# A streaming logsumexp on one core: tiles 42 to 53 weighed and summed by fused VectorE steps, and one wide constant matmul in place of three narrow ones

## The chip, the cores and the metric

The kernel runs on one core of a Trainium2 chip. The time is the device time of one execution in microseconds (us); what is compared is the median of several executions. The names used below are those of the profile: PE is TensorE's matmul, PEld its weight load, DVE is VectorE, ACT is ScalarE, POOL is GpSimd, SP is the SyncE queue that issues the DMAs.

## The reference

```python
# x: (8, 2048, 2048) float32, bias: (8, 256) float32; H = 8 heads of Dh = 256
x_heads = x.reshape(B, S, H, Dh).transpose(0, 2, 1, 3) + bias[None, :, None, :]
x_tiled = np.repeat(x_heads, 2, axis=2)          # each row twice
mx = x_tiled.max(axis=-1, keepdims=True)
lse = mx.squeeze(-1) + np.log(np.exp(x_tiled - mx).sum(axis=-1))   # (8, 8, 4096)
```

For every row of 2048 numbers there are eight sums of 256 exponentials, and the logarithm of each. The kernel leaves the maximum out, since the inputs are small; it checks at its end that no sum went out of range, and has a second, slow path for that case, which is not taken here.

## The kernel before

The input, 134 MB, is streamed through SBUF once, in 64 tiles of 2 MB: 128 partitions, K = 2 rows each, 2048 columns. There are eight tile buffers (NBUF). Tile t uses buffer t mod 8, and the load of tile t + 8 is issued by SP (`load`, L174 and L186) once the last user of tile t is done; the list `last_uses` says who that is. Loads are of two tiles (4 MB) up to tile 41 and of one tile or less after it. From tile 57 on a tile is loaded and worked by single rows, called units here; the last tile comes in eight pieces of columns (`LAST_COLS`).

The order of the work on every engine is the order in which the program emits it; nothing is reordered. `STAGES` gives each tile a mode. In a mode, `pe` is the number of heads whose bias TensorE adds, `g0` is the head from which GpSimd adds the bias, `acc` is the number of heads whose sum ScalarE makes itself while it takes the exponential, and heads from `pe` to `g0` get no bias at all: their exponentials are multiplied by exp(bias) afterwards, which is meant by "weighed". `fold` heads are weighed and half summed by GpSimd.

- BULK, tiles 0 to 53. TensorE puts the bias of heads 0 to 2 into PSUM (`put_bias`, L303) and adds x to it through a matmul on the identity (`late_heads`, L362). ScalarE takes the exponential of head 0 with its sum (L373) and of heads 1 and 2 without (L380). GpSimd adds the bias to heads 4 to 7 in place (`g_add`, L412). One tile later, in `later`, ScalarE takes the exponential of heads 3 to 7 in place (L418), VectorE multiplies head 3 of both rows by its factor (L430) and then sums heads 1 to 7 of both rows in one reduction of 3584 elements per partition (L437).
- MIXED, tiles 54 to 56. Head 0 goes through TensorE (`add_x`, L338; ScalarE L393). Heads 1 to 3 are weighed and summed by one fused VectorE step for each head and row (`weigh`, L453: multiply by the factor and accumulate). Heads 4 to 7 go as in BULK, but with a reduction of 2048 elements.
- Units of tiles 57 to 63. No GpSimd addition; TensorE takes the first heads, `weigh` the middle ones, and GpSimd weighs and folds the last one or two (`fold`, L469 and L477), which a short reduction finishes (L483).

At tile 54 `first_factors` makes the factors of heads 1 and 2 in the bank `one_ps`: TensorE spreads the bias over the partitions (L235) and ScalarE takes the exponential (L268). On TensorE this follows the bias matmul of tile 55, and on ScalarE it stands ahead of everything of tile 54.

From tile 57 on, `keep_warm` (L353) issues NWARM = 3 matmuls of the identity with itself for each unit, into the bank `tp`, where nobody reads them. `finish` transposes the sums of a batch into `tp` (L497), ScalarE takes their logarithm (L507); `finish_last` (L606, L612) does so for the last batch, and `ends_of` and `judge` (L525 to L550) test the range.

Of the kernel before, what the change touches and what calls it, by code (L numbers as in the profile page):

```python
# [13 lines left out]
ALU = mybir.AluOpType  # L14
# [7 lines left out]
NBUF = 8  # L22

NEARLY = 5

NWARM = 3

# [1 line left out]

BULK = dict(pe=3, acc=1, g0=4, late=True, fold=0)
MIXED = dict(pe=1, acc=1, g0=4, late=False, fold=0)
PROMPT_F1 = dict(pe=2, acc=2, g0=8, late=False, fold=1)
PROMPT_F2 = dict(pe=2, acc=2, g0=8, late=False, fold=2)
# [9 lines left out]

STAGES = [
    (0, (BULK,)),
    (54, (MIXED,)),  # L50
    (57, (PROMPT_F1, PROMPT_F1)),
    (62, (SINGLE_F1, SINGLE_F1)),
# [10 lines left out]
def kernel(  # L63
# [6 lines left out]
    nc = tc.nc  # L70
    P = nc.NUM_PARTITIONS
    B, S, D = x.shape
    H, Dh = bias.shape
# [2 lines left out]
    NB = S // (P * KB)  # L76
    TB = KB // K
    T = B * NBLK
    T_PROMPT = STAGES[1][0]
    T_FACTORS = T // 2  # L80
    CPE = BULK["pe"] * Dh
    MM = 512


    V0, W0, G0, W1, W2 = Dh, 3 * Dh, 4 * Dh, 6 * Dh, 7 * Dh
# [30 lines left out]
    xts = [xb[:, k : k + K] for xb in xbs for k in range(0, KB, K)]  # L116
    w_ps = pp.tile([P, W2 - W0], F32, name="w_ps")
# [5 lines left out]
    tp = pp.tile([P, KB, P], F32, name="tp")  # L123
# [41 lines left out]
    last_uses = [[] for _ in range(T)]  # L165
# [73 lines left out]
    for i, c in enumerate(range(G0, D, MM)):  # L239
        spread(ps[i], c, c + MM)  # L240
        nc.vector.tensor_copy(b_rep[:, c - G0 : c - G0 + MM], ps[i])
    W_LATE = BULK["g0"] * Dh
    w_late = w_ps[:, 0 : W_LATE - W0]
# [7 lines left out]
        out=b_far,  # L251
        in_=brow,
        op=ALU.max,
        axis=mybir.AxisListType.X,
# [3 lines left out]
        out=Rx[0][0:1, 1 + NR :],  # L258
# [90 lines left out]
        return heads  # L349

    def keep_warm():
        for _ in range(NWARM):
            nc.tensor.matmul(  # L353
                tp[:, 0], lhsT=ident, rhs=ident, start=True, stop=True
            )

    def late_heads(m, t, got, sums):


        mms = []  # L360
        for h, p in enumerate(got[:-1]):
            mm = nc.tensor.matmul(  # L362
                p,
                lhsT=ident,
                rhs=xts[t % NBUF][:, :, h * Dh : (h + 1) * Dh],
                start=False,
                stop=True,
            )
            mms.append(on_x(t, mm, [loads[t, 0, 0]]))

        def pe_part():
            for k in range(K):
                act = nc.scalar.activation(  # L373
                    out=xts[t % NBUF][:, k, 0:Dh],
                    in_=got[0][:, k * Dh : (k + 1) * Dh],
                    func=ACT.Exp,
                    accum_out=sums[:, k, 0:1],
                )
                last_uses[t].append(on_x(t, act, [mms[0]]))
            act = nc.scalar.activation(  # L380
                out=xts[t % NBUF][:, :, Dh : m["pe"] * Dh].rearrange(
                    "p k (h j) -> p h k j", j=Dh
                ),
                in_=got[-1].rearrange("p (h k j) -> p h k j", k=K, j=Dh),
                func=ACT.Exp,
            )
            on_x(t, act, [mms[-1]])

        return pe_part

# [26 lines left out]
    def exp_inplace(t, v, after):  # L417
        return on_x(t, nc.scalar.activation(out=v, in_=v, func=ACT.Exp), [after])  # L418

    def later(m, t, k0, k1, sums, add):  # L420

        h0 = m["pe"] if m["late"] else m["g0"]
        v = xts[t % NBUF][:, k0:k1, h0 * Dh : D]
        done = exp_inplace(t, v, add)
        if m["late"]:
            n = (m["g0"] - h0) * Dh
            f = v[:, :, 0:n]
            h0 = m["acc"]
            v = xts[t % NBUF][:, k0:k1, h0 * Dh : D]
            mul = nc.vector.tensor_tensor(  # L430
                out=f,
                in0=f,
                in1=each_row(w_ps, m["pe"] * Dh - W0, n, k1 - k0),
                op=ALU.mult,
            )
            done = on_x(t, mul, [done])
        red = nc.vector.tensor_reduce(  # L437
            out=sums[:, k0:k1, h0:H],
            in_=v.rearrange("p k (h j) -> p k h j", j=Dh),
            op=ALU.add,  # L440
            axis=mybir.AxisListType.X,
        )
        last_uses[t].append(on_x(t, red, [done]))

    def weigh(t, v, h, dst, after):
        c = h * Dh
        if c < W0:
            w = one_ps[:, c - V0 : c - V0 + Dh]
        elif c < W2:
            w = w_ps[:, c - W0 : c - W0 + Dh]  # L450
        else:
            w = w_sb[:, c - W1 : c - W1 + Dh]
        ttr = nc.vector.tensor_tensor_reduce(  # L453
            out=v,
            in0=v,
            in1=w,
            scale=1.0,
            scalar=0.0,
            op0=ALU.mult,
            op1=ALU.add,  # L460
            accum_out=dst,
        )
        last_uses[t].append(on_x(t, ttr, [after]))
# [181 lines left out]
    for t in range(T):  # L645
        if t == T_FACTORS:
            other_factors()
        xt = xts[t % NBUF]
        sums = sums_of(t)
        for k0, k1, c0, c1 in pieces(t):  # L650
            m = modes_of(t)[k0]
            add = None
            heads = []
            if c0 == 0:
                bias_here = bias_there
            if m["late"]:
                pe_part = late_heads(m, t, bias_here, sums)
            else:
                heads = add_x(m, t, k0, c0, c1, bias_here)

                def pe_part(t=t, heads=heads, sums=sums):
                    for k, h, bank, p, mm in heads:
                        sum_biased(t, k, h, bank, p, mm, sums)

            if c0 == 0:
                if next_units and not m["late"]:
                    bias_there = put_bias(*next_units.pop(0))
                if t > T_PROMPT and m["g0"] == H:
                    keep_warm()
                if m["g0"] < H:  # L670
                    add = g_add(m, t, k0, k1)
                if t < T - 1 or k0 == 0:
                    flush(for_pool)
            if t == T_PROMPT and (k0, c0) == (0, 0):
                first_factors()
            h0 = max(c0 // Dh, m["pe"])
            h1 = min(c1 // Dh, m["g0"])
            hf = max(h0, min(h1, H - m["fold"]))
            if h0 < h1 and not m["late"]:
                done = exp_inplace(  # L680
                    t, xt[:, k0:k1, h0 * Dh : h1 * Dh], loads[t, k0, c0]
                )
# [14 lines left out]

            def pool_part(t=t, m=m, k0=k0, k1=k1, sums=sums, add=add):
                if add:
                    later(m, t, k0, k1, sums, add)  # L700
# [56 lines left out]
```

## Time and profile before

| what | value |
|---|---|
| median of 3 runs | 326.36 us (325.95 to 326.98) |
| the profiled execution | 327.41 us, its span 325.5 us |
| DVE busy | 289.4 us, 89% of the span |
| POOL busy | 287.5 us, 88% |
| PE busy | 272.7 us, 84% |
| ACT busy | 265.6 us, 82% |
| DMA | 135.44 MB, mean 416 GB/s, 98.0% of 16 engines' span on the load queue |

The span is the time from the first to the last instruction of the program on the core; 1.9 us of the profiled execution's own time lie outside it. Four engines and the DMA are all busy for more than four fifths of the span, so shares alone do not tell which of them sets the end: that has to be read from the chain of waits and from the stretches late in the trace.

### The profile page before, as it was taken

The page shows a single profiled execution, that of the slowest core. Times are in us where ns is not written, and L with a number is a line of the kernel's source. Part 1 is how long each engine was busy: PE and PEld are TensorE (multiplying, and loading weights), DVE is VectorE, ACT ScalarE, POOL GpSimd, SP SyncE. Part 2 cuts the span into 40 slices and gives each one's busy share as a digit, 9 for nine tenths or more (in the row PEclk, how much of TensorE's full clock was granted, in tenths as well). Part 3 has the DMA queues.
Part 4 walks back from the last instruction along what each step waited for, and adds up shares of the span by engine and source line. Part 5 has one row for each costly group of instructions (what it writes and reads, how often), then busy time and mean ns, then how long its engine had stood idle before and what let it go on. Part 6 is the DMA issues. An engine that isn't in the chain of part 4 may idle for free.

```text
span 325.5 us, 2458 instructions
## 1 busy us (share of the span) xinstructions
PE 272.7 (84%) x695; PEld 102.8 (32%) x695; DVE 289.4 (89%) x329; ACT 265.6 (82%) x426; POOL 287.5 (88%) x120
## 2 busy tenths in 40 slices
PE   5999999878898869888688878698999786598983
PEld 2333333322233323332233323233333232135451
DVE  1346879999999998989989999969999999999996
ACT  1157789898598987889889979869899699989993
POOL 6939997999999899999999999999999999858872
PEclk9977899999597997979899979778999799589999
DMA  8999999999999999999999999999999999999992
GB/s 307 464 403 439 451 417 420 447 439 407 443 443 408 437 435 431 423 439 432 419 443 434 415 443 431 407 433 427 427 421 430 429 424 424 417 421 415 421 391 93
DMA packets 8832, 135.44 MB, mean 416 GB/s; under 512 B 1041, under 2 KB 1425, under 8 KB 2417
## 3 DMA queue, kind: packets, MB, share of 16 engines
q1 hardware_dynamic: 8720, 135.27, 98.0%
q8 instruction: 5, 0.08, 0.1%
q14 instruction: 9, 0.07, 0.1%
q10 hardware_dynamic: 98, 0.01, 0.0%
HBM read 134.23 MB, written 1.05 MB: 416 GB/s over the span
## 4 chain that ended last, share of the span: by engine, by line
DVE 43%; DMA 26%; PE 18%; ACT 8%; POOL 3%; issue 0%; SPq 0%; DVEq 0%
DVE R L437 28%; DMA xb<-in_x_dram 26%; DVE xb L453 9%; PE pair L362 7%; ACT xb L418 6%; DVE xb L430 4%; PE one_ps L362 4%; POOL xb L412 3%; PE pair L303 3%; PE one_ps L303 2%; PE pair L235 1%; ACT xb L380 1%; ACT xb L373 1%; DMA brow<-in_bias_dram 1%; ACT res L507 1%
## 5 line engine op out<-in xcount | busy, mean ns | idle before, releaser
L412 POOL TENSOR_TENSOR xb<-xb,b_rep 128x2048 f32<-128x2048 f32 x57 | 257.3, 4537 | 21.3 <-DMA xb<-in_x_dram 21.1
L437 DVE TENSOR_REDUCE R<-xb 128x14 f32<-128x3584 f32 (+1 forms) x57 | 216.8, 3804 | 1.9
L418 ACT ACTIVATE xb<-xb 128x2560 f32<-128x2560 f32 (+5 forms) x77 | 157.5, 2055 | 8.2 <-POOL xb L412 8.0
L362 PE MATMUL pair<-xb,ident 128*128 128x512 f32 x216 | 117.3, 671 | 0.0
L362 PE MATMUL one_ps<-xb,ident 128*128 128x512 f32 x108 | 68.1, 716 | 10.9 <-DMA xb<-in_x_dram 10.9
L380 ACT ACTIVATE xb<-pair 128x1024 f32<-128x1024 f32 x54 | 56.0, 1038 | 25.0 <-PE pair L362 25.0
L362 PEld LDWEIGHTS pair<-xb,ident 128*128 128x128 f32 x216 | 47.0, 218 | 62.6 <-issue 62.6
L430 DVE TENSOR_TENSOR xb<-xb,w_ps 128x512 f32<-128x512 f32 x54 | 36.8, 681 | 24.0 <-ACT xb L418 23.9
L373 ACT ACTIVATE xb<-one_ps 128x256 f32<-128x256 f32 x108 | 40.4, 387 | 6.7 <-PE one_ps L362 6.7
L303 PEld LDWEIGHTS <-ones 3*128 3x128 bf16 (+1 forms) x192 | 16.8, 95 | 78.0 <-issue 69.0
L303 PE MATMUL one_ps<-b,ones 3*128 3x512 bf16 x49 | 19.1, 390 | 20.9 <-ACT xb L373 20.9
L303 PE MATMUL pair<-b,ones 3*128 3x512 bf16 x98 | 29.1, 376 | 0.0
L362 PEld LDWEIGHTS one_ps<-xb,ident 128*128 128x128 f32 x108 | 17.2, 201 | 33.7 <-DMA xb<-in_x_dram 17.3
L338 PE MATMUL pair<-xb,ident 128*128 128x512 f32 (+1 forms) x36 | 20.5, 656 | 6.3 <-DMA xb<-in_x_dram 6.3
L373 ACT ACTIVATION_READ_ACCUMULATOR xb<-one_ps 128x1 f32 x108 | 23.0, 213 | 0.0
L453 DVE CUSTOM_DVE_ANT_0 xb<-xb,w_ps 128x256 f32<-128x256 f32 x61 | 22.3, 416 | 0.0
L477 POOL TENSOR_TENSOR xb<-xb 128x128 f32<-128x128 f32 (+3 forms) x39 | 13.9, 357 | 3.1
L469 POOL TENSOR_TENSOR xb<-xb,w_sb 128x256 f32<-128x256 f32 (+1 forms) x13 | 10.0, 772 | 5.2 <-ACT xb L418 4.6
L353 PE MATMUL tp<-ident 128*128 128x128 f32 x84 | 13.0, 291 | 0.9 <-ACT res L507 0.9
L507 ACT ACTIVATE res<-tp 32x1024 f32<-32x1024 f32 x7 | 7.1, 1011 | 6.2 <-PE tp L497 6.2
L393 ACT ACTIVATE xb<-pair 128x256 f32<-128x256 f32 x33 | 12.0, 368 | 0.0
L353 PEld LDWEIGHTS tp<-ident 128*128 128x128 f32 x84 | 10.5, 191 | 4.3 <-issue 2.8
(55 smaller groups left out, 91.8 us busy)
## 6 DMA issues: line engine op xcount, KB each, us to landing
xb<-in_x_dram SPq DMA_DIRECT2D x20, 4096.0 KB, 21.3
xb<-in_x_dram SPq DMA_DIRECT2D x17, 2048.0 KB, 22.0
xb<-in_x_dram SPq DMA_DIRECT2D x12, 1024.0 KB, 21.3
xb<-in_x_dram SPq DMA_DIRECT2D x4, 256.0 KB, 13.3
out_dram<-res SPq DMA_DIRECT2D x1, 896.0 KB, 6.8
xb<-in_x_dram SPq DMA_DIRECT2D x2, 384.0 KB, 15.9
xb<-in_x_dram SPq DMA_DIRECT2D x2, 128.0 KB, 6.4
out_dram<-res_last SPq DMA_DIRECT2D x1, 128.0 KB, 1.7
```

What stands on the lines that cost most here:

```text
L303: nc.tensor.matmul(p, lhsT=lhsT, rhs=each_row(b, h * Dh, Dh, K), start=i == 0, stop=False,)
L338: mm = nc.tensor.matmul(p, lhsT=ident, rhs=xts[t % NBUF][:, ka:kb, c : c + w], start=False, stop=True,)
L353: nc.tensor.matmul(tp[:, 0], lhsT=ident, rhs=ident, start=True, stop=True)
L362: mm = nc.tensor.matmul(p, lhsT=ident, rhs=xts[t % NBUF][:, :, h * Dh : (h + 1) * Dh], start=False, stop=True,)
L373: act = nc.scalar.activation(out=xts[t % NBUF][:, k, 0:Dh], in_=got[0][:, k * Dh : (k + 1) * Dh], func=ACT.Exp, accum_out=sums[:, k, 0:1],)
L380: act = nc.scalar.activation(out=xts[t % NBUF][:, :, Dh : m["pe"] * Dh].rearrange("p k (h j) -> p h k j", j=Dh), in_=got[-1].rearrange("p ...
L412: add = nc.gpsimd.tensor_tensor(out=v, in0=v, in1=each_row(b_rep, c - G0, D - c, k1 - k0), op=ALU.add)
L418: return on_x(t, nc.scalar.activation(out=v, in_=v, func=ACT.Exp), [after])
L430: mul = nc.vector.tensor_tensor(out=f, in0=f, in1=each_row(w_ps, m["pe"] * Dh - W0, n, k1 - k0), op=ALU.mult,)
L437: red = nc.vector.tensor_reduce(out=sums[:, k0:k1, h0:H], in_=v.rearrange("p k (h j) -> p k h j", j=Dh), op=ALU.add, axis=mybir.AxisListTy ...
L453: ttr = nc.vector.tensor_tensor_reduce(out=v, in0=v, in1=w, scale=1.0, scalar=0.0, op0=ALU.mult, op1=ALU.add, accum_out=dst,)
L477: done = nc.gpsimd.tensor_tensor(out=v[:, :, 0:n], in0=v[:, :, 0:n], in1=v[:, :, n : 2 * n], op=ALU.add)
```

## The change

A new mode CATCH takes tiles 42 to 53. It is BULK with `fused=True`. In `later`, the one multiplication and the one reduction of 3584 elements become: a reduction of heads 1 and 2 (1024 elements), which waits only for ScalarE's exponential of these heads (L380, handed over in `pe_done`); two fused `weigh` steps for head 3, one for each row; and a reduction of heads 4 to 7 (2048 elements). TensorE, ScalarE and GpSimd do the same as before for these tiles.

`keep_warm` now issues one matmul of the identity on 384 columns of `b_rep` (float32) in place of three on 128 columns, and it is called once for each row of a unit from tile 54 on: so the three MIXED tiles, which had none, get two each, and the units from tile 57 on one each. At tile 54 the two stand on TensorE ahead of the spreading of `first_factors`.

```diff
-NWARM = 3
+WARM = 384
-BULK = dict(pe=3, acc=1, g0=4, late=True, fold=0)
+BULK = dict(pe=3, acc=1, g0=4, late=True, fused=False, fold=0)
+CATCH = dict(pe=3, acc=1, g0=4, late=True, fused=True, fold=0)
 STAGES = [
     (0, (BULK,)),
+    (42, (CATCH,)),
     (54, (MIXED,)),
...
     def keep_warm():
-        for _ in range(NWARM):
-            nc.tensor.matmul(
-                tp[:, 0], lhsT=ident, rhs=ident, start=True, stop=True
-            )
+        nc.tensor.matmul(
+            tp.rearrange("p k q -> p (k q)")[:, 0:WARM],
+            lhsT=ident,
+            rhs=b_rep[:, 0:WARM],
+            start=True,
+            stop=True,
+        )
...
-            on_x(t, act, [mms[-1]])
+            pe_done.append(on_x(t, act, [mms[-1]]))
...
+    def add_up(t, k0, k1, h0, h1, sums, after):
+        red = nc.vector.tensor_reduce(
+            out=sums[:, k0:k1, h0:h1],
+            in_=xts[t % NBUF][:, k0:k1, h0 * Dh : h1 * Dh].rearrange(
+                "p k (h j) -> p k h j", j=Dh
+            ),
+            op=ALU.add,
+            axis=mybir.AxisListType.X,
+        )
+        last_uses[t].append(on_x(t, red, [after]))
+
+    def later(m, t, k0, k1, sums, add, pe_done):
+        xt = xts[t % NBUF]
         h0 = m["pe"] if m["late"] else m["g0"]
-        v = xts[t % NBUF][:, k0:k1, h0 * Dh : D]
-        done = exp_inplace(t, v, add)
-        if m["late"]:
+        done = exp_inplace(t, xt[:, k0:k1, h0 * Dh : D], add)
+        if not m["late"]:
+            add_up(t, k0, k1, m["g0"], H, sums, done)
+        elif m["fused"]:
+            add_up(t, k0, k1, m["acc"], m["pe"], sums, pe_done[0])
+            for k in range(k0, k1):
+                for h in range(h0, m["g0"]):
+                    v = xt[:, k, h * Dh : (h + 1) * Dh]
+                    weigh(t, v, h, sums[:, k, h : h + 1], done)
+            add_up(t, k0, k1, m["g0"], H, sums, done)
+        else:
...
-                if t > T_PROMPT and m["g0"] == H:
-                    keep_warm()
+                if t >= T_PROMPT:
+                    for _ in range(k1 - k0):
+                        keep_warm()
```

`T_PROMPT` stays at 54 (it is now read from the third stage).

More of the change, by code (lines that the diff above doesn't have):

```diff
@@ L78 @@
     T = B * NBLK
-    T_PROMPT = STAGES[1][0]
+    T_PROMPT = STAGES[2][0]
     T_FACTORS = T // 2
@@ L351, in keep_warm, with late_heads @@
     def keep_warm():
-        for _ in range(NWARM):
-            nc.tensor.matmul(
-                tp[:, 0], lhsT=ident, rhs=ident, start=True, stop=True
-            )
-    def late_heads(m, t, got, sums):
+        nc.tensor.matmul(
[5 more added lines that the diff above has]
+        )
+    def late_heads(m, t, got, sums, pe_done):
         mms = []
@@ L418, in exp_inplace @@
         return on_x(t, nc.scalar.activation(out=v, in_=v, func=ACT.Exp), [after])
-    def later(m, t, k0, k1, sums, add):
-        h0 = m["pe"] if m["late"] else m["g0"]
-        v = xts[t % NBUF][:, k0:k1, h0 * Dh : D]
-        done = exp_inplace(t, v, add)
-        if m["late"]:
+    def add_up(t, k0, k1, h0, h1, sums, after):
[10 more added lines that the diff above has]
+        xt = xts[t % NBUF]
+        h0 = m["pe"] if m["late"] else m["g0"]
+        done = exp_inplace(t, xt[:, k0:k1, h0 * Dh : D], add)
[9 more added lines that the diff above has]
+        else:
             n = (m["g0"] - h0) * Dh
-            f = v[:, :, 0:n]
-            h0 = m["acc"]
-            v = xts[t % NBUF][:, k0:k1, h0 * Dh : D]
+            f = xt[:, k0:k1, h0 * Dh : h0 * Dh + n]
             mul = nc.vector.tensor_tensor(
@@ L432, in later @@
                 in0=f,
-                in1=each_row(w_ps, m["pe"] * Dh - W0, n, k1 - k0),
+                in1=each_row(w_ps, h0 * Dh - W0, n, k1 - k0),
                 op=ALU.mult,
             )
[L436 to L443, printed above, removed]
+            add_up(t, k0, k1, m["acc"], H, sums, on_x(t, mul, [done]))
     def weigh(t, v, h, dst, after):
@@ L653 @@
             heads = []
+            pe_done = []
             if c0 == 0:
@@ L656 @@
             if m["late"]:
-                pe_part = late_heads(m, t, bias_here, sums)
+                pe_part = late_heads(m, t, bias_here, sums, pe_done)
             else:
@@ L696, with pool_part @@
                         )
-            def pool_part(t=t, m=m, k0=k0, k1=k1, sums=sums, add=add):
+            def pool_part(
+                t=t, m=m, k0=k0, k1=k1, sums=sums, add=add, pe_done=pe_done
+            ):
                 if add:
-                    later(m, t, k0, k1, sums, add)
+                    later(m, t, k0, k1, sums, add, pe_done)
                 if k1 == K:
```

## The prediction

> **What bounds the kernel now.** I first read the chain that ended last, on the page. Its engine line:
>
> ```profile
> DVE 43%; DMA 26%; PE 18%; ACT 8%; POOL 3%; issue 0%; SPq 0%; DVEq 0%
> ```
>
> VectorE holds the largest share, but a chain over the whole span mixes stages. So the second view is VectorE's waits from 233 to 322 us:
>
> ```profile
> DVE xb L430 <- ACT xb L418: 0.2, 1, 0.2
> ```
>
> That 0.2 us belongs to the multiplication of tile 43 at 232.65; after it VectorE waits for nobody until the last sum stands. Its timeline at the end:
>
> ```profile
> 320.85 0.42 DVE L453 CUSTOM_DVE_ANT_0 xb<-xb,w_sb 128x256 f32<-128x256 f32 x1
> ...
> 321.19 0.22 DVE L483 TENSOR_REDUCE R<-xb 128x2 f32<-128x64 f32 x1
> 321.52 0.29 DVE L525 TENSOR_REDUCE ends<-R 128x1 f32<-128x129 int32 x1
> ```
>
> The sums are complete at 321.41; PE's last transpose starts at 321.56, the span ends at 325.47, so 4.06 us of fixed tail follow. The third view is the table of stretches, which tells what the others do then (fields: PE, PEld, DVE, ACT, POOL busy, granted clock, DMA share, GB/s):
>
> ```profile
> 287.00:312.00 25.00, 22.67 (x102) 12.02 (x101) 25.00 (x128) 24.50 (x50) 18.07 (x41) 1.00 1.01 416
> 312.00:318.00 6.00, 5.23 (x26) 3.02 (x26) 6.00 (x38) 5.93 (x18) 4.82 (x10) 1.00 1.05 381
> 318.00:320.00 2.00, 0.87 (x6) 0.46 (x5) 2.00 (x14) 1.91 (x8) 1.44 (x3) 1.00 0.59 195
> ```
>
> The DMA is full until 318 and then drains: the last load lands at 318.15. ScalarE is nearly as full as VectorE. So VectorE sets the end, but not by much; the fourth view, the ends of ScalarE and GpSimd, says by how much:
>
> ```profile
> 319.67 0.24 ACT L393 ACTIVATION_READ_ACCUMULATOR xb<-pair 128x1 f32 x1
> ```
> ```profile
> 317.93 1.67 POOL L477 TENSOR_TENSOR xb<-xb 128x256 f32<-128x256 f32 x3
> ```
>
> ScalarE's last sum stands at 319.91, GpSimd's last fold at 319.60. This is the ceiling on any gain of VectorE's.
>
> **Part 1, the fused steps.** The rows by form:
>
> ```profile
> L437 DVE TENSOR_REDUCE R<-xb 128x14 f32<-128x3584 f32 x54 | 210.0, 3888 | 1.9
> L430 DVE TENSOR_TENSOR xb<-xb,w_ps 128x512 f32<-128x512 f32 x54 | 36.8, 681 | 24.0 <-ACT xb L418 23.9
> L437 DVE TENSOR_REDUCE R<-xb 128x8 f32<-128x2048 f32 x3 | 6.9, 2284 | 0.0
> ```
>
> Before, multiplications of consecutive tiles start 4.52 us apart (237.18, 241.69, 246.21). After: the two reduction rows differ by 1.604 us for 1536 elements, 1.04 ns each, so one of 1024 elements takes about 1.21 us and holds the engine some 0.08 less, 1.13 (the 2048 form lasts 2.28 and starts its follower after 2.20). Fused steps follow each other every 0.34. Sum: 1.13 + 2 x 0.34 + 2.20 = 4.01, a saving of 0.51 per tile, 6.1 us over twelve. The pessimistic bound uses whole durations, with nothing overlapped: before 0.68 + 3.89 = 4.57; after 1.21 + 2 x (0.42 + 0.08) + 2.28 = 4.49; 0.08 per tile, 1.0 in all. I take 0.51, since the step-to-step times are rows of the same instructions back to back.
>
> [...]
>
> What becomes of 6.1 us? VectorE was behind: tile 53 is multiplied at 278.20, while its exponential ended at 275.08, so it can gain no more than its lag and then waits for ScalarE. With heads 1 and 2 summed early, tile 53 needs 2 x 0.34 + 2.20 = 2.88 behind 275.08, and ends at 278.0 instead of 282.7. From there I walk the old ScalarE times. The reductions of tiles 54 and 55 need exponentials that end about 280 and 284.4; that of tile 56 starts at 287.50 and lasts 1.92, so VectorE ends it at 291.6 instead of 295.5. A unit costs VectorE 1.80 and ScalarE 2.09 (exponentials start at 297.86, 299.95, 302.04), so VectorE then keeps close behind ScalarE. At the end: exponentials of the last unit finish at about 317.85, 318.3 and 318.75; VectorE has two, two and one head to weigh, ends these at 319.8, then the short reduction behind GpSimd's 319.60: 320.0. So the sums stand at 320.0 instead of 321.41: 1.4 us. The other 4.7 only turn into waiting. The early release of buffers (loads wait for L437) brings nothing: loads already lie some 22 us in the queue, with the DMA share at 1.0.
>
> Even 0.12 us per tile pays for the whole 1.4, so the size of the saving matters little. The extra wait for L380 stands ahead of L418 on ScalarE and holds nothing back.
>
> **Part 2, the constant matmuls.** In the units, six passes of 128 columns start at 0.13 apart (0.77 per unit); two passes of 384, scaled from two of 512 (L338 at 314.59 to L320 at 315.55, 0.96), take 0.72. No difference.
>
> At tile 54 two matmuls, four passes, 4 x 0.36 = 1.44 us at full clock, stand ahead of the spreading. On ScalarE, L268 and all of tile 54 queue behind that:
>
> ```profile
> 274.36 1.02 PE L235 MATMUL one_ps<-brow,ones 1*128 1x512 f32 x2
> ...
> 275.48 0.58 ACT L268 ACTIVATE one_ps<-one_ps 128x512 f32<-128x512 f32 x1 [0.40 <-PE one_ps L235]
> ```
>
> The cover: ScalarE later waits for GpSimd twice, 0.44 at 282.51 and 0.98 at 287.50, 1.42 together. So 1.44 is just absorbed, with nothing left. Behind 287.50 ScalarE has hardly a gap until it waits for the load of tile 62's second row at 312.85 (about 0.2): a later start at 287.50 is carried to the end, less 0.2. If the clock is at half there, the cost is larger. The stretches in steps of 3.4 us:
>
> ```profile
> 269.60:273.00 3.40, 2.19 (x6) 0.66 (x4) 3.37 (x2) 3.38 (x7) 3.11 (x1) 1.00 1.00 424
> 273.00:276.40 3.40, 2.37 (x6) 0.69 (x5) 3.37 (x3) 3.00 (x3) 3.36 (x1) 1.00 0.99 419
> 276.40:279.80 3.40, 1.87 (x2) 0.50 (x2) 3.37 (x3) 3.40 (x6) 3.01 (x2) 0.50 0.99 412
> ```
>
> PE was at full clock at 274 and fell to half at 276.4. Without the old 2.17 us stall at 255.81 (L507 waiting for transposes that waited for VectorE's sums) ScalarE and PE run earlier, so PE waits more for loads near 270, and the half clock may begin sooner. One stretch of it loses 1.7 us of PE work.
>
> [...] I take full clock for the likeliest case and charge 0.2 for jitter.
>
> Sum: 1.4 - 0.2 = 1.2 us. Profiled execution 327.41 to 326.2; median 326.36 to 325.2 (0.37%). About 0.3%, 1.0 us, can be told from no change. The profiled execution is 1.05 slower than the median; if that excess is VectorE's lag, a median execution has a margin of only 1.4 - 1.05 = 0.35.
>
> **Rivals.**
> 1. The end is already near the floor of the loads: gain 0.3 to 0.9, 325.5 to 326.1. For it: the three runs spread over 1.0 us. Against: VectorE's unbroken 88 us.
> 2. Half clock in one stretch at tile 54: spreading late by 1.44 + 1.7 = 3.1, ScalarE late by 3.1 - 1.42 = 1.7 at 287.5 and by 1.5 at the end: sums at 321.4, no gain, 326.4.
> 3. Slower: the half clock lasts two stretches there. ScalarE late by 3.4 at 287.5, sums at 319.9 + 3.2 = 323.1, 1.7 later than now: 328.1. It decides from a delay of the spreading above 1.42 + 0.2 + 1.5 = 3.1 us. Against: the added matmuls themselves keep PE busy.
> 4. The split saves nothing, below the 1.0 us bound: VectorE unchanged, 326.4.
>
> **How the numbers follow.** Likeliest case 0.49 (324.3 to 325.4), rival 1 0.20, rival 2 0.15, rival 3 0.12, rival 4 0.04. Rival 1 lies mostly within 0.3%. Faster 0.52, same 0.36, slower 0.12. The range 324.3 to 327.0 leaves out most of rival 3 and a little below.
>
> **What would show it.** Right: L437 of 1024 elements near 1.2 us in tiles 42 to 53, steps 4.0 us apart or waits of VectorE for L418; L268 idle before it about 1.9 instead of 0.40; L418 of tile 56 still at about 287.5; sums complete near 320.0 with ScalarE, GpSimd and VectorE ending together. Wrong: L418 of tile 56 beyond 289 with PEclk 0.50 at 273, or a last landing other than 318.

## The result, and the profile after

| | before | after |
|---|---|---|
| median | 326.02 us (325.80 to 326.98, 13 runs) | 327.88 us (327.18 to 331.24, 13 runs) |
| ratio after / before | | 1.0075, 95% interval 1.0054 to 1.0096 |
| the profiled execution | 327.41 us, span 325.5 us | 328.98 us, span 326.8 us |
| VectorE instructions | 329 | 377 |

The kernel became slower by 1.9 us, where 1.2 us less had been forecast; the time lies above the range (324.3 to 327.0) as well. Of the 1.9, about 1.6 are in the span (its median is 325.7, and 324.1 to 324.4 in the batches of before below) and about 0.3 outside it. Two executions of the last batch below, one of before (422.87 us) and one of e10 (494.69 us), were in a far slower state and are left out of the ratios.

**The engine line of the chain that ended last**, on the page of after. VectorE's share fell to less than half, and the DMA leads:

```profile
DMA 33%; ACT 23%; PE 23%; DVE 18%; POOL 1%; issue 1%; SPq 0%; DVEq 0%; ACTq 0%
```

**The waits of VectorE, 225 to 326 us** (us in total, times, longest). In before there was one of 0.2 after 233; now VectorE has caught up and waits for ScalarE:

```profile
DVE xb L468 <- ACT xb L423: 6.0, 5, 3.2
```

**The waits of ScalarE, 270 to 326 us.** The 0.40 us that ScalarE waited for the spread bias at tile 54 have become 4.2, and a new wait, for TensorE's adding to tile 53, stands before it:

```profile
ACT one_ps L270 <- PE one_ps L237: 4.2, 1, 4.2
ACT xb L385 <- PE pair L367: 1.8, 1, 1.8
```

**TensorE's timeline at tile 54** (start, duration). The constant matmuls (L354) stand ahead of the spreading (L237), and both run at half clock: four passes take 2.58 us instead of the estimated 1.44 (1.56 at full clock, in e2 below), and the spreading 2.07 where it took 1.02 before.

```profile
275.30 2.58 PE L354 MATMUL tp<-b_rep,ident 128*128 128x384 f32 x4
277.81 2.07 PE L237 MATMUL one_ps<-brow,ones 1*128 1x512 f32 x2
```

**ScalarE's timeline**, at tile 54 and at the end. The factors' exponential starts at 279.98 instead of 275.48, and the last sum stands at 322.49 instead of 319.91:

```profile
279.98 0.58 ACT L270 ACTIVATE one_ps<-one_ps 128x512 f32<-128x512 f32 x1 [4.18 <-PE one_ps L237]
...
322.30 0.19 ACT L398 ACTIVATION_READ_ACCUMULATOR xb<-pair 128x1 f32 x1
```

**VectorE's timeline at the end.** The sums are complete at 322.67 instead of 321.41:

```profile
322.46 0.21 DVE L498 TENSOR_REDUCE R<-xb 128x2 f32<-128x64 f32 x1
```

**The table of stretches** (PE, PEld, DVE, ACT, POOL busy, granted clock, DMA share, GB/s). TensorE is at about half clock from 276 to 287 and still never idle; from 287 to 312 it is ScalarE that is busy without a gap, not VectorE. From 318 to 320 the DMA share is 0.87, where it was 0.59:

```profile
276.00:287.00 11.00, 11.00 (x16) 3.68 (x16) 7.43 (x19) 7.02 (x13) 10.14 (x3) 0.55 1.01 418
287.00:312.00 25.00, 22.34 (x56) 8.63 (x55) 24.61 (x125) 25.00 (x50) 15.68 (x36) 0.93 1.01 417
...
318.00:320.00 2.00, 2.00 (x6) 1.02 (x6) 2.00 (x12) 2.00 (x7) 1.78 (x4) 1.00 0.87 232
```

That last figure points to a second change: the last load lands at 319.00 instead of 318.15. In this execution nothing waits for it: from 300 to 322 us no engine waits for a load, since ScalarE, late from tile 54, comes to every load after it has landed. In before, TensorE's waits from 300 to 322 us were:

```profile
PE pair L338 <- DMA xb<-in_x_dram: 1.4, 4, 0.8
```

Whether the late landing costs time by itself has to come from kernels in which tile 54 is not late. **The DMA view of 311 to 314 us** has a packet in it that does not belong to the loads; it is an 8 KB read of instructions (of VectorE's, as e5 below shows), and starts at 312.27:

```profile
q14 instruction: 1, 0.01, 0.7%
```

In before, the view of 319 to 320.5 us has it; it starts at 319.67, when the last load has landed:

```profile
q14 instruction: 1, 0.01, 1.3%
```

In both kernels it comes when VectorE has run about 317 recorded instructions; the change adds 48 ahead of it (four for each of twelve tiles: one more reduction, and two fused steps with a read of the accumulator each in place of one multiplication), and so the read moves in among the loads. How much this costs, and through what, is what the experiments settle.

### The profile page after: what moved, and what is told of

Its sections match the earlier page's. It is cut to its first block, busy times and chain, and to the rows that moved or that the text cites. A ratio compares the mean times of both kernels' runs of the same rounds, so it can differ in the third digit from the quotient of the medians.

```text
span 326.8 us, 2418 instructions
## 1 busy us (share of the span) xinstructions
PE 277.3 (85%) x651; PEld 101.7 (31%) x651; DVE 285.2 (87%) x377; ACT 265.6 (81%) x426; POOL 287.5 (88%) x120
## 3 DMA queue, kind: packets, MB, share of 16 engines
HBM read 134.23 MB, written 1.05 MB: 414 GB/s over the span
## 4 chain that ended last, share of the span: by engine, by line
DMA 33%; ACT 23%; PE 23%; DVE 18%; POOL 1%; issue 1%; SPq 0%; DVEq 0%; ACTq 0%
DMA xb<-in_x_dram 33%; ACT xb L423 15%; DVE R L426 14%; PE pair L367 9%; PE one_ps L367 4%; PE pair L305 3%; ACT xb L398 3%; DVE xb L468 2%; ACT xb L385 2%; PE one_ps L305 2%; DVE xb L452 2%; ACT res L522 1%; POOL xb L417 1%; PE pair L237 1%; ACT xb L378 1%; PE tp L512 1%
## 5 line engine op out<-in xcount | busy, mean ns | idle before, releaser
L426 DVE TENSOR_REDUCE R<-xb 128x14 f32<-128x3584 f32 (+2 forms) x69 | 211.2, 3073 | 2.4 <-ACT xb L385 0.6
L367 PE MATMUL pair<-xb,ident 128*128 128x512 f32 x216 | 118.6, 677 | 0.0
L367 PE MATMUL one_ps<-xb,ident 128*128 128x512 f32 x108 | 66.4, 699 | 10.3 <-DMA xb<-in_x_dram 10.3
L452 DVE TENSOR_TENSOR xb<-xb,w_ps 128x512 f32<-128x512 f32 x42 | 28.6, 681 | 22.2 <-ACT xb L423 22.2
L468 DVE CUSTOM_DVE_ANT_0 xb<-xb,w_ps 128x256 f32<-128x256 f32 x85 | 31.4, 415 | 2.9 <-ACT xb L423 2.8
L354 PE MATMUL tp<-b_rep,ident 128*128 128x384 f32 x40 | 20.5, 613 | 2.7 <-ACT res L522 2.7
L378 ACT ACTIVATION_READ_ACCUMULATOR xb<-one_ps 128x1 f32 x108 | 22.1, 205 | 0.0
L340 PE MATMUL pair<-xb,ident 128*128 128x512 f32 (+1 forms) x36 | 19.5, 625 | 0.0
L468 DVE CUSTOM_DVE_ANT_0 xb<-xb,one_ps 128x256 f32<-128x256 f32 x27 | 10.6, 413 | 3.3 <-ACT xb L423 3.2
```

Of the source, the lines that this page charges most:

```text
L340: mm = nc.tensor.matmul(p, lhsT=ident, rhs=xts[t % NBUF][:, ka:kb, c : c + w], start=False, stop=True,)
L354: nc.tensor.matmul(tp.rearrange("p k q -> p (k q)")[:, 0:WARM], lhsT=ident, rhs=b_rep[:, 0:WARM], start=True, stop=True,)
L367: mm = nc.tensor.matmul(p, lhsT=ident, rhs=xts[t % NBUF][:, :, h * Dh : (h + 1) * Dh], start=False, stop=True,)
L378: act = nc.scalar.activation(out=xts[t % NBUF][:, k, 0:Dh], in_=got[0][:, k * Dh : (k + 1) * Dh], func=ACT.Exp, accum_out=sums[:, k, 0:1],)
L426: red = nc.vector.tensor_reduce(out=sums[:, k0:k1, h0:h1], in_=xts[t % NBUF][:, k0:k1, h0 * Dh : h1 * Dh].rearrange("p k (h j) -> p k h j" ...
L452: mul = nc.vector.tensor_tensor(out=f, in0=f, in1=each_row(w_ps, h0 * Dh - W0, n, k1 - k0), op=ALU.mult,)
```

## The experiments

Three batches of runs, each beside the kernel before on the same chip. "Read" is the start of the 8 KB instruction read that comes between VectorE's 306th and 323rd recorded instruction (e11 has only 287, and no such read before 327), "landed" the end of the last load, "sums" the time at which all sums stand; these three come from the profiled execution and the rest from all executions.

| run | median (before) | ratio [95%] | read | landed | sums |
|---|---|---|---|---|---|
| before, profiled | 326.02 | | 319.67 | 318.15 | 321.41 |
| after | 327.88 (326.02) | 1.0075 [1.0054, 1.0096] | 312.27 | 319.00 | 322.67 |
| e1_fused_only | 327.73 (326.07) | 1.0078 [1.0043, 1.0112] | 309.57 | 319.19 | 325.23 |
| e2_warm_only | 327.38 (326.07) | 1.0034 [1.0017, 1.0050] | 319.30 | 318.09 | 319.96 |
| e3_spread_first | 327.26 (326.07) | 1.0048 [1.0020, 1.0075] | 309.67 | 318.97 | 321.71 |
| e4_factors_early | 335.80 (326.07) | 1.0291 [1.0274, 1.0308] | 317.15 | 318.89 | 329.12 |
| e5_before_padded | 327.47 (325.97) | 1.0068 [1.0035, 1.0101] | 309.94 | 318.93 | 321.73 |
| e6_fused_51 | 326.48 (325.97) | 1.0015 [1.0006, 1.0023] | 316.76 | 319.03 | 320.57 |
| e7_paired | 326.46 (325.97) | 1.0015 [1.0004, 1.0026] | 319.76 | 318.39 | 320.28 |
| e8_paired_spread_first | 326.62 (325.97) | 1.0018 [1.0006, 1.0029] | 319.57 | 318.18 | 320.06 |
| e9_before_again | 325.84 (one execution) | | 319.12 | 318.05 | 319.92 |
| e10_paired_change | 327.75 (326.23) | 1.0031 [1.0014, 1.0047] | 319.66 | 318.01 | 323.01 |
| e11_paired_only | 329.56 (326.23) | 1.0102 [1.0078, 1.0127] | none | 318.07 | 323.21 |
| e12_change_again | 327.72 (one execution) | | 311.21 | 318.97 | 321.44 |

### The two parts by themselves, and the order at tile 54 (e1, e2, e3)

The first theory was that of rival 3: the spreading comes too late on TensorE, and that is all.

e1_fused_only keeps the fused tiles and takes the constant matmuls of before:

```diff
-        nc.tensor.matmul(tp.rearrange("p k q -> p (k q)")[:, 0:WARM],
-                         lhsT=ident, rhs=b_rep[:, 0:WARM], ...)
+        for _ in range(3):
+            nc.tensor.matmul(tp[:, 0], lhsT=ident, rhs=ident, ...)
...
-                if t >= T_PROMPT:
-                    for _ in range(k1 - k0):
-                        keep_warm()
+                if t > T_PROMPT and m["g0"] == H:
+                    keep_warm()
```

> The fused steps in tiles 42 to 53 alone; the constant matmuls are as before (three of 128 columns for each unit from tile 57 on, none in the mixed tiles). Theory A (the two constant matmuls that stand on TensorE ahead of the spreading at tile 54 make ScalarE late, nothing else does): the spreading follows its bias matmul at once, L268 starts near 275.5, the sums are complete near 320.0, time 324.7 to 325.5. Rival B (the fused tiles let PE run into waits for loads, which halves the clock near 270 whatever the constant matmuls do, and so delays tile 54): 326.0 to 328, with a wait of ScalarE for the spreading of over 2 us. Rival C (fused steps save nothing): 326.0, as before.

Measured: 327.73 us (327.10 to 331.40, 12 runs), as slow as the whole change, without a single constant matmul at tile 54. The theory that the constant matmuls ahead of the spreading are all of it fell here. The last load landed at 319.19 instead of 318.15. ScalarE's wait for the spreading was still 2.3 us, though the matmuls ahead of it were those of before. ScalarE came there no earlier (275.00 us, 275.08 before), but TensorE's clock was at half from 273.1, where in before it fell at 276.4, and the spreading started 0.9 us later and took 1.91 us instead of 1.02. This is rival B of the expectation:

```profile
275.28 1.91 PE L237 MATMUL one_ps<-brow,ones 1*128 1x512 f32 x2
```

e2_warm_only has the opposite part:

```diff
-    (42, (CATCH,)),
...
-T_PROMPT = STAGES[2][0]
+T_PROMPT = STAGES[1][0]
```

> The wide constant matmuls alone, also between the mixed tiles; no fused tiles. Theory A: the spreading is late by 1.4 to 4.9 us by the clock it meets. ScalarE has 1.4 of cover behind it and another 1.5 to VectorE's end, so 326.0 at full clock and up to 328 at half clock; the executions spread more than those of before. Rival B (the fused tiles are the cause): 326.0, as before, within 0.2.

Measured: 327.38 us (325.90 to 328.42, 8 runs). The profiled execution happens to be the fastest of them, 325.90, and shows ScalarE waiting 2.0 us for the spreading at full clock, absorbed later, with the last load at 318.09. So this part costs about 1.1 us by the ratio, but not in every execution. That it leaves the landing of the loads alone is seen in this one execution, which lost nothing; e10 below has a slow one.

e3_spread_first has the whole change, with the constant matmuls behind the spreading:

```diff
-                if t >= T_PROMPT:
-                    for _ in range(k1 - k0):
-                        keep_warm()
...
             if t == T_PROMPT and (k0, c0) == (0, 0):
                 first_factors()
+            if c0 == 0 and t >= T_PROMPT:
+                for _ in range(k1 - k0):
+                    keep_warm()
```

> The changed kernel whole, but at every unit the constant matmuls are issued behind the spreading instead of ahead of it; only tile 54 has one, so only there the order differs. Theory A: L268 waits for the spreading no more than 1 to 2 us, L418 of tile 56 at 287.5, time 324.7 to 325.6. Rival B (half clock from the fused tiles): 326.5 to 328. Rival D (the wide constant matmuls or the ones of tiles 55 and 56 cost time themselves): 327 to 328, as the changed kernel.

Measured: 327.26 us (327.01 to 331.29, 9 runs). ScalarE's wait for the spreading is back at 0.4 (its waits, 270 to 326 us):

```profile
ACT one_ps L270 <- PE one_ps L237: 0.4, 1, 0.4
```

Yet the last load still landed at 318.97, and the time stayed 1.2 us above before. This was above what theory A had (324.7 to 325.6). Two causes, then: the late spreading, and something with the loads that goes with the fused tiles.

### The factors earlier (e4)

e4_factors_early computes the factors of heads 1 and 2 at tile 36 and keeps them in SBUF, which takes the spreading out of tile 54 altogether:

```diff
+    v_sb = sb.tile([P, W0 - V0], F32, name="v_sb")
...
-        spread(one_ps, V0, W0)
-        nc.scalar.activation(out=one_ps, in_=one_ps, func=ACT.Exp)
+        flat = tp.rearrange("p k q -> p (k q)")
+        spread(flat, V0, W0)
+        nc.scalar.activation(out=v_sb, in_=flat, func=ACT.Exp)
...
+        if t == T_FACTORS + 4:
+            first_factors()
```

> The changed kernel, but the factors of heads 1 and 2 are made at tile 36 through the bank tp into SBUF, so that neither the spreading nor its exponential stands at tile 54. Theory A: no wait and 0.5 us less of ScalarE at tile 54, time 324.5 to 325.4. Rival B: 326 to 328, since PE's slow matmuls still delay tile 54's own first head. Rival D: 327 to 328.

Measured: 335.80 us, a loss of 9.7 us that neither theory had. The groups by form show where: on average a fused step costs twice as much with the factor in SBUF as with it in PSUM (instructions; busy us, mean ns; idle before):

```profile
L470 DVE CUSTOM_DVE_ANT_0 xb<-xb,w_ps 128x256 f32<-128x256 f32 x85 | 31.3, 411 | 2.9 <-ACT xb L425 2.9
L470 DVE CUSTOM_DVE_ANT_0 xb<-xb,v_sb 128x256 f32<-128x256 f32 x27 | 22.8, 864 | 0.0
```

The timelines of VectorE and GpSimd show that it is not the step itself. One of these steps with the factor in SBUF, started at 282.80 while GpSimd was idle, lasted 0.41 us; the next one lasted 4.40, from 283.49, behind a GpSimd addition that had started at 283.04. Between them, at 283.15, a step with its factor in PSUM took 0.41 us beside the same addition:

```profile
283.49 4.40 DVE L470 CUSTOM_DVE_ANT_0 xb<-xb,v_sb 128x256 f32<-128x256 f32 x1
```
```profile
283.04 4.56 POOL L419 TENSOR_TENSOR xb<-xb,b_rep 128x2048 f32<-128x2048 f32 x1 [0.45 <-DMA xb<-in_x_dram]
```

This run tells nothing of the disputed causes, but it shows what it is worth that the factors are in PSUM: 411 ns a step on average instead of 864.

### The instruction read (e5, e6)

e5_before_padded is the kernel before with 48 VectorE instructions of one element ahead of the first tile, where they hold up nothing. If the loads are late because buffers are released at other times, or because of TensorE's clock, nothing changes; if it is the read, its place moves as in the changed kernel:

```diff
+    pad = sb.tile([1, 1], F32, name="pad")
+    for _ in range(48):
+        nc.vector.memset(pad, 0.0)
     for t in range(T):
```

> The kernel before, with 48 one-element VectorE memsets ahead of the first tile, which change no work of the tiles. They bring VectorE's instruction count to that of the changed kernel. Theory F (the 8 KB instruction read that follows VectorE's 317th instruction falls behind the loads before the change, at 319.7, and among them after it, at 309 to 312, and holds one of the sixteen DMA engines for about 1 us): that read comes near 311, the last load lands near 319.1 instead of 318.15, and the time is 326.8 to 327.2 or above. Rival E (the loads land late because buffers are released earlier): landing 318.15 and time 326.0, since no buffer is released earlier here. Rival P (only the half clock of PE matters): 326.0.

Measured: 327.47 us (327.09 to 331.10, 9 runs): 1.5 us slower, with no change in the work on the tiles. The DMA view of 309 to 311 us has the read:

```profile
q14 instruction: 1, 0.01, 1.0%
```

The page's DMA issues (KB each, median us from issue to landing) of before, then of e5. Loads of three sizes take longer to land: by 0.9 us those of 256 KB and 384 KB, by 0.5 those of 128 KB, of which the last is also issued 0.8 later:

```profile
xb<-in_x_dram SPq DMA_DIRECT2D x4, 256.0 KB, 13.3
...
xb<-in_x_dram SPq DMA_DIRECT2D x2, 384.0 KB, 15.9
xb<-in_x_dram SPq DMA_DIRECT2D x2, 128.0 KB, 6.4
```
```profile
xb<-in_x_dram SPq DMA_DIRECT2D x4, 256.0 KB, 14.2
...
xb<-in_x_dram SPq DMA_DIRECT2D x2, 384.0 KB, 16.8
xb<-in_x_dram SPq DMA_DIRECT2D x2, 128.0 KB, 6.9
```

The trace says how 8 KB can cost a microsecond. Every load is split over 16 DMA engines, which are not in step. These are the ends of their sixteen parts in us after the eighth, in after, for the last load that the read did not touch and for the second one behind it:

```
load issued 290.29: -0.84 -0.78 -0.72 -0.70 -0.66 -0.61 -0.58 0.00 0.07 0.64 0.71 0.72 0.91 1.03 1.17 1.18
load issued 295.28: -0.83 -0.79 -0.71 -0.69 -0.65 -0.61 -0.58 0.00 0.06 0.63 0.71 0.72 0.95 1.03 1.22 2.13
```

Fifteen parts end as before; one, of the engines that were last anyway, falls back by 0.95 us, and stays there up to the last load: its fifteenth part ended at 318.01 in before and at 318.03 in after, its sixteenth, with which the load has landed, at 318.15 and 319.00.

How 0.9 us at the landing become 1.5 us of the time can be read from two stretches of e5 (fields as above). In the first, TensorE waits for late loads and is busy for 2.12 of the 4 us, where it was 3.04 in e9, an ordinary execution of before. Then its clock is at half for one step of 3.4 us, where e9 has full clock:

```profile
310.00:314.00 4.00, 2.12 (x11) 1.43 (x11) 4.00 (x27) 2.98 (x8) 3.18 (x8) 1.00 1.01 391
314.00:318.00 4.00, 4.00 (x12) 1.98 (x11) 3.12 (x21) 3.52 (x7) 2.36 (x5) 0.57 1.04 346
```

From 306 to 322 us ScalarE waits 1.0 us for a load and 0.7 for TensorE, and the sums stand 2.8 us behind the landing instead of the 1.9 of e9. The profiled execution of e3 has the same: 2.07 us, then a step at half clock, and ScalarE's waits are 0.8 and 0.7.

e6_fused_51 fuses only tiles 51 to 53, so that there are 12 more instructions instead of 48:

```diff
-    (42, (CATCH,)),
+    (51, (CATCH,)),
```

> Fused steps in tiles 51 to 53 alone, constant matmuls as before: 12 more VectorE instructions instead of 48, and a saving of 3 x 0.5 us. Theory F: the read after the 317th instruction comes near 317, so it can only touch the very last loads: landing at most 0.9 late, time 326.0 to 326.8. Rival E: hardly any earlier release, landing 318.15, 325.0 to 326.0. Rival P: 326 to 327.5 by the clock at tile 54.

Measured: 326.48 us (326.34 to 326.68, 11 runs), read at 316.76. Only the last loads come after it. The last one landed as late as in after (319.03), but ScalarE had by then been served in time, the clock was full to the end, and the sums stood 1.5 us behind the landing. This fits a cost that depends on how many loads follow the read: 0.5 us here, 1.5 us in e5. It is not shown by this alone, since e6 has three fused tiles as well and e5 has none.

### The fused steps without the read (e7, e8, e10, e11)

e7_paired has fused tiles 44 to 53 and the old constant matmuls, and gets the instructions back elsewhere: of tiles 0 to 41, which are loaded in pairs, two that were loaded together share one multiplication and one reduction, which makes 327 VectorE instructions instead of 377.

```diff
+    def later_paired(m, t, k0, k1, add):
+        done = exp_inplace(t, xts[t % NBUF][:, k0:k1, h0 * Dh : D], add)
+        if t % TB < TB - 1:
+            return
+        mul = nc.vector.tensor_tensor(out=f, in0=f, in1=each_row(...), op=ALU.mult)
+        red = nc.vector.tensor_reduce(out=R[b][:, :, m["acc"] : H, blk // TB],
+                                      in_=xb[:, :, m["acc"] * Dh :]..., op=ALU.add, ...)
...
-    (42, (CATCH,)),
+    (44, (CATCH,)),
```

> Fused steps in tiles 44 to 53, constant matmuls as before, and VectorE's multiplication and reduction of tiles 0 to 43 done for two tiles at once where tiles come in pairs (tiles 0 to 41), so that VectorE has two instructions fewer than before the change, and buffers of tiles 44 to 53 are still released early. Sums are moved one tile later to the transposes for the paired tiles. Theory F: the read of the 317th instruction falls behind the last load again, landing near 318.15, fast executions at 325.8 to 326.1 instead of the 327.1 of the fused tiles alone. Rival E: landing 319, 327.1. Rival P: spread as with the fused tiles alone, 327 to 331.

Measured: 326.46 us (325.69 to 327.83, 11 runs). With the read back at 319.76 the loads landed at 318.39, and no execution came near the 331 us that after, e1, e3 and e5 reach. But it is no faster than before, and 0.4 us above the range of theory F; about 0.25 us of its excess over before lie outside the span.

e8_paired_spread_first is e7 with the wide constant matmuls behind the spreading, as in e3.

> As the kernel with paired tiles, with the wide constant matmuls also between the mixed tiles, but behind the spreading at tile 54. Theory F, with the half clock as the second cause: landing near 318.15 and a denser PE, 325.5 to 326.1, with fewer executions far above. Rival E: 327. Rival P: 325.5 to 326, as the clock is then full at the end.

Measured: 326.62 us (326.05 to 327.87, 11 runs), 0.18% above before and above the 326.1 that theory F allowed. Its profiled execution has the loads (318.18) and sums (320.06) of an ordinary execution of before.

e10_paired_change is e8 with the order of the change at tile 54: the constant matmuls ahead of the spreading.

> The whole change (wide constant matmuls ahead of the spreading at tile 54) with VectorE's steps of tiles 0 to 43 paired and fused tiles from 44 on: the instruction read at the end is taken away, the late spreading stays. If both causes are there and add: above the paired kernel with the spreading first (326.62) by 0.3 to 1.0, and below the change (327.88) by 0.5 to 1.0: 326.9 to 327.5, landing near 318.2. If the instruction read is all: 326.5.

Measured: 327.75 us (326.21 to 329.24, leaving out 494.69). Nothing but that order lies between e8 and e10, but they were run in different batches: by the medians e10 is 1.1 us above e8, by the ratios to their own before (1.0031 and 1.0018) only 0.4 us, and the intervals overlap. So the size is open. The way is seen in the profiled execution, the slowest of the eleven (329.24 us); ScalarE's waits, 270 to 326 us:

```profile
ACT one_ps L274 <- PE one_ps L241: 5.3, 1, 5.3
```

The last load landed at 318.01, with the read behind it, and the sums still stood only at 323.01. This is rival 3 by itself, in one execution.

e11_paired_only pairs the steps of tiles 0 to 41 and fuses nothing.

> The kernel before with VectorE's steps of tiles 0 to 43 paired, nothing else: 42 VectorE instructions fewer, no fused tiles. It is the control of the paired kernels. If the pairing itself costs what these lie above before: 326.4. If it is free: 325.9 to 326.1, and then the 0.45 us of the paired kernel with fused tiles are theirs. The 317th instruction is reached after the last load in either case, landing near 318.1.

Measured: 329.56 us (329.17 to 331.06, 6 runs). That is far above both cases of the expectation. The pairing makes VectorE late, and the sums stand at 323.21 while ScalarE's last stands at 320.50. From e11 to e7 the fused tiles gain 2.8 us, each against its own before (3.1 by the bare medians): the fused steps do shorten a kernel, where VectorE is what is late.

### Both kernels once more (e9, e12)

> The kernel before, profiled once more. Its median is 326.0 us, and the execution that the prediction argued from took 327.41. Theory G (an ordinary execution of before already ends at the floor that the last load sets, and the profiled one was late by 1.4 us): time near 326.0, last load near 318.1, sums complete at 320.0 to 320.2 instead of 321.41. Rival (VectorE is always the last by 1.4 us): sums 1.3 us or more behind ScalarE's last.

Measured: 325.84 us. The last steps of ScalarE and VectorE:

```profile
319.54 0.24 ACT L393 ACTIVATION_READ_ACCUMULATOR xb<-pair 128x1 f32 x1
```
```profile
319.70 0.22 DVE L483 TENSOR_REDUCE R<-xb 128x2 f32<-128x64 f32 x1
```

ScalarE's last sum stands at 319.78, VectorE's at 319.92, as theory G had it. The last load landed at 318.05, only 0.10 earlier than in the profiled execution that the prediction went by (318.15), but there the sums stood at 321.41.

> The changed kernel, profiled once more: an execution from the lower group (327.2 to 327.9) has the late landing (near 319) with PE at full clock from 287 on; one from the upper group (near 331) has a half clock stretch of PE in the last 15 us beside it, with ScalarE waiting for PE there by 3 to 4 us.

Measured: 327.72 us. ScalarE waited 3.7 us for the spreading, the last load landed at 318.97, the sums stood at 321.44. Against e9 the sums are 1.5 us later, and 0.4 us more lie outside the span. The landing is 0.92 later, as expected, but it is not what is paid for here: as in the profiled execution of after, no engine waits for a load from 300 to 322 us. The exponential of tile 56 already starts 1.85 us later than in e9 (289.11 and 287.26). Nor was the clock full from 287 on, as expected: it was at half from 293.9 to 300.7.

## Why the prediction was wrong, point by point

**"VectorE sets the end, but not by much": a reading of one execution.** The page was of an execution 1.05 us above the median of the three runs shown. In e9 and e2, at 325.84 and 325.90, the sums are complete at 319.92 and 319.96, which is where the prediction put them after the change (320.0). In e9 VectorE and ScalarE already end together, 1.9 us behind the last load: without waiting for VectorE the sums would have stood 0.14 us earlier (319.78). So rival 1 was the true picture of before, as far as one execution of e9 shows it. The text had worked this out ("a margin of only 1.4 - 1.05 = 0.35") and charged the full 1.2 us to the median all the same. That step failed: the excess of the execution should have come off before the gain was counted.

**Part 1, the saving per tile: right.** Fused steps of consecutive tiles start 4.00 us apart, against 4.01 in the sum and 4.52 before. VectorE's timeline, the first step of head 3 in tiles 42 and 43:

```profile
227.28 0.41 DVE L468 CUSTOM_DVE_ANT_0 xb<-xb,w_ps 128x256 f32<-128x256 f32 x1
...
231.28 0.41 DVE L468 CUSTOM_DVE_ANT_0 xb<-xb,w_ps 128x256 f32<-128x256 f32 x1
```

The reduction of 1024 elements, by form, lasts the 1.21 us of the estimate:

```profile
L426 DVE TENSOR_REDUCE R<-xb 128x4 f32<-128x1024 f32 x12 | 14.5, 1210 | 0.6 <-ACT xb L385 0.6
```

So 0.52 us per tile were saved (4.52 less 4.00). That the saved time turns into waiting for ScalarE was right too (6.0 us).

**"The early release of buffers brings nothing": the loads were taken as fixed.** The loads land late in e5 too, where no buffer is released earlier; so it is not the release that moves them. The prediction named "a last landing other than 318" as a sign that it was wrong, but had no term for it. It counted the instructions that VectorE runs and not that they are read by DMA. A view of before had the clue: one read of 8 KB at 319.67, 1.5 us behind the last load, that 48 more instructions must pull forward. The term is 0.85 us at the landing. By e5 it is worth 1.5 us of the time where nothing else is late; in the two profiled executions of the changed kernel, where no load is waited for after 300 us, what is late within the span comes from tile 54.

VectorE itself did not wait for the read: its waits from 225 us on go back to ScalarE, GpSimd and TensorE in after, and to ScalarE and TensorE in e5. The loads were late behind it, though it is one read of 8192 bytes: the last one landed at 318.93 in e5 instead of 318.15, and the kernel was slower by 1.5 us.

**Part 2, the cover at tile 54: the clock and the margin.** "So 1.44 is just absorbed, with nothing left" was charged at full clock as the likeliest case. No run shows the 0.2 us that were charged for jitter; what the runs showed in its place is a wait that differed by up to 3.3 us with the same order at tile 54. ScalarE's wait for the spreading was 4.2 (after), 3.7 (e12), 2.0 (e2) and 5.3 us (e10) instead of 1.9. In e2 all of it ran at full clock (1.56 us for the four passes, 1.12 for the spreading), and the cover did hold: the exponential of tile 56 started at 287.42. In e12 the clock was at half for one stretch of 3.4 us, in which most of the constant matmuls fell (2.29 us):

```profile
273.40:276.80 3.40, 3.40 (x6) 0.98 (x5) 3.01 (x7) 1.70 (x1) 3.40 (x1) 0.50 0.99 417
```

In after and e10 it was at half for three and four such stretches, and the spreading ran at half clock too. So both rivals with the half clock had the mechanism, with chances of 0.15 and 0.12. Rival 2 had the exponential of tile 56 late by 1.7 us and the sums at 321.4; in e12 it is 1.6 (289.11 instead of 287.50) and 321.44. Rival 3 had 3.4 us and 323.1; in e10 it is 3.2 and 323.01, in after 2.8 (290.33) and 322.67. That the price of rival 3, 328.1 us, lies near the median of after, 327.88, is in part luck: the executions differ (e12, at 327.72, is of rival 2's kind, the one at 328.98 of rival 3's), and about 0.3 us of the loss lie outside the span. The prediction's own view showed the clock falling to half at 276.4, and the text itself said that PE's waits near 270 might bring that sooner. It came sooner: at 273.4 in e12, at 273.0 in e10, and from 268.9 to 272.3 and 275.7 to 285.9 in after. TensorE was busy for 1.71 us of 270.0 to 273.4 in e12 and for 2.19 of 269.6 to 273.0 in before, which agrees; that the waits brought the half clock is argued and not shown. The sign that the prediction had named, the exponential of tile 56 beyond 289, came in both profiles of the changed kernel. So the step that failed here is the full clock at tile 54. Rival 4 is refuted by the 4.00 us.

**The matmul widths, "no difference": right.** e8 and e7 differ by 0.16 us with the constant matmuls off the path of the spreading.

**How the causes add up.** They do not. By medians against their own before, the instruction read alone costs 1.5 us (e5), the fused tiles with it 1.7 (e1), the constant matmuls alone 1.3 (e2; 1.1 by the ratio), and all together 1.9. The profiles say why: in after, e12 and e10 ScalarE is so late from tile 54 that no load is waited for after 300 us, while in e3 and e5, where the spreading is on time, TensorE waits 2.4 us for loads there (1.4 in before). The delay at tile 54 hides the one of the loads. Without the read and with the spreading first (e8), 0.65 us are left, of which 0.3 lie outside the span.

**The executions near 331 us.** After has three of 13 above 330.9, e1 five of 12, e3 one of nine, e5 two of nine. One of them was profiled, in e1 (331.40 us). The stretches of its tail:

```profile
310.00:314.00 4.00, 1.96 (x11) 1.22 (x10) 2.88 (x17) 3.11 (x10) 2.49 (x6) 1.00 1.00 390
314.00:324.00 10.00, 10.00 (x28) 5.75 (x29) 6.88 (x41) 6.80 (x18) 5.43 (x11) 0.50 0.62 192
```

With the loads late, TensorE is busy for only half of 310 to 314; the clock is halved for the ten microseconds that follow, three steps where e3 and e5 had one, and ScalarE then waits for TensorE:

```profile
ACT xb L395 <- PE pair L340: 4.0, 3, 1.9
```

These four are the kernels with the read between 309 and 313 us; e2, e6, e7 and e8, which have it at 316.76 or later, stay below 328.5. (e10 and e11, late for other reasons, reach 329.24 and 331.06.) That the other executions near 331 have the same trace is likely, but they were not profiled.

**What stays open.** The time outside the span is 2.1 to 2.2 us by the medians in after, e1, e3, e4, e5, e7, e8, e10 and e11, and 1.8 to 1.9 in before, e2 and e6. It goes neither with the number of VectorE instructions nor with the constant matmuls, and no run settles it. Why the profiled execution of before was 1.5 us later at the sums than e9 is open as well. Nor was a version found that beats the kernel before.

## What to carry to other kernels

Before a gain at the end is counted, compare the profiled execution with the median: what it is late by is not there to be saved, and here that was nearly all of it. In a kernel whose DMA is full up to the end, look up in the DMA view where the instruction reads fall, and count how far added instructions move them towards the last loads: here one read of 8192 bytes among them put the last landing back by 0.85 us (after). And work put ahead of something that others wait for should be priced at the slow clock (in after 2.58 us for four passes at half clock, 1.56 at full clock at 286.77), or simply be put behind it: the constant matmuls alone, ahead of the spreading, cost 0.34% (e2), and with the order turned ScalarE's wait there was 0.4 us (e3) instead of 3.7 and 4.2.

## What the runs showed of the hardware

- Instruction reads of 8192 bytes put one of the 16 DMA engines back by 0.7 to 1.0 us (three reads among the loads in before, four in after), although the packet of a read among the loads took 0.31 to 0.41 us itself. At the read of 312.27 in after the other fifteen went on as before, and the one it met was one of those that were behind: every later load was late, the last one by 0.85 us (319.00, 318.15 in before). A read at 295.88 in before met one that was ahead: its part went from 0.46 to 1.43 us after the eighth, and the last one stayed at 1.62. So a read among the loads did not always cost.
- A VectorE instruction with both inputs in SBUF (the fused step with `v_sb`, in e4) lasted 0.41 us when it started with GpSimd idle, and 4.40 us behind a GpSimd addition of 4.56 us, 0.29 us after which it ended; with the factor in PSUM its mean was 0.41 in the same kernel, and 0.41 beside that very addition.
- The granted clock changed in steps of 3.41 us: in before and after it stayed the same for 3.41 to 47.8 us at a time, always a multiple of that, up to 323 us. In after TensorE was busy at half clock without a gap for 10.2 us (275.7 to 285.9) before the full clock was granted again.
